# Softmax attention's output computed already turned, its gate turned beforehand, with some PSUM tiles in other banks

## The chip, the cores and the metric

The kernel runs on one core of a Trainium2 chip. The metric is the device time of one execution in microseconds (us), given as the median of the runs. The core's engines run side by side and meet through semaphores: PE (TensorE, matrix products), PEld (its weight loads), DVE (VectorE), ACT (ScalarE), POOL (GpSimd) and SP (SyncE, which here only issues DMAs).

## The reference, cut to what matters

Two decoder layers over 256 tokens of width 1024. Each layer normalises x, multiplies it by one input projection whose 4096 columns are eight groups of 512 (MQ, MK, MV, MZ for softmax attention with 4 heads of 128; RQ, RK, RV, RZ for retention with 4 heads of 128), gates both results with SiLU, multiplies them by an output projection, adds x, and then adds a gated per-layer embedding. With 256 tokens there is one attention block, so the softmax attention is plain causal attention:

```python
pr = softmax(q_m @ k_m.T + bias, causal)       # per head, 256 x 256
m_out = silu(mz) * (pr @ v)                    # per head, 256 x 128
y = concat([r_out, m_out]) @ w_out[i]          # r_out: retention, gated alike
x = x + y
x = x + sigmoid(rms_norm(x) @ w_ple_gate[i]) * rms_norm(p[i] @ w_ple[i], ple_norm_g[i])
```

## The kernel before, in words

**Products.** PE takes a stationary operand of 128 x 128 and a moving one of up to 512 columns. The large products are made of three products of split numbers: each number is a high part (`hi`, type fp32r) and a low part (`lo`, the remainder), and hi·hi, hi·lo and lo·hi are summed in PSUM (`mm3`, lines 405 to 407). Some small products are done in one fp32 product instead, which the profile shows as two records each (lines 950, 960, 1010). Products of split numbers in the attention and retention scores go through `three` (line 932): three records of 256 columns each.

**Weights.** A `Stage` is half of a 512 x 512 weight block's rows in two chunks. Each chunk is loaded by SP (line 340), cast to `hi` by ACT (line 350) and split to `lo` by DVE (line 353), and then used by four `hi`·`lo` products on PE (two row blocks k, two token halves m). There are 95 such chunks; 8 staging buffers and 5 pairs of split buffers hold them, and later in each layer the tiles T, V, G, PS and K2 are lent as further pairs.

**Turning.** A result with tokens on the partitions is wanted with features on the partitions before the next product. `halves` (line 621, ACT) separates the 16-bit halves of the fp32 numbers, `turned` (line 631) lets SP issue a DMA transposition, and two DVE copies (line 640, one for each 16-bit half) put the halves together again. `to_parts` (line 643) does this and then makes `hi` (ACT, line 657) and `lo` (DVE, line 659).

**Order.** The order of the instructions on every engine is fixed when the program is built. A planner (`Flow`) keeps a clock for each engine, takes a cost in us for each step (`ask`), and issues the step that can start first, among several the one with the earliest due time; `LIFT` adds an offset to the due time of chains that it names. The large products follow each other in the order MQ, MK, RQ, RK, MZ, MV, RV, RZ, then the output projection, the embedding (`embed`) and the gate. The small products of attention are `groups` that are put between them (`tick`) when what they need has been ready for a margin and enough `mix` banks are free: `moba_scores`, `moba_out` with `ret_scores_own`, `ret_scores`, `ret_out`.

**Softmax attention.** `moba_scores` makes scores in three tiles; `probs` adds the bias, takes the exponential (sums in `DEN`), and turns the result into `PT` (tile PS), keys on the partitions. `value` copies the projection MV, scaled, to `V`. `moba_out` then calls `pv` for each half m of the tokens: `PT` is stationary, `V` moves, and the output has tokens on the partitions, 12 fp32 products of 128 columns a layer (line 960). `moba_y` multiplies by the gate `G` and by 1/`DEN` with four DVE instructions (line 978), and `to_parts` turns the result and splits it into `yT`, parts 4 to 7, which the output projection reads first. Parts 0 to 3 come from the retention group (`ret_gate`).

**PSUM.** Eight banks: four named `acc` and four named `mix`. The output projection takes all four `acc`, the embedding `mix`.

Of the kernel before, what the change touches and what calls it, by code (L numbers as in the profile page):

```python
# [18 lines left out]
P = 128  # L19
D = 1024  # L20
S = 256
# [37 lines left out]
TURN = 0  # L59
AHEAD = 1.6  # L60
# [5 lines left out]
LIFT = {("gen", 38): 4.0, ("rope", 3): -7.0, ("gen", 4): -4.0, ("gate", 1): 1.0, ("hr1", 3): 2.0}  # L66
# [188 lines left out]
def tile_hybrid_trunk(ctx: ExitStack, tc: tile.TileContext, early, x, pT, ple_g, rel_bias,  # L255
# [332 lines left out]
    L_X = flow.begin(load(lambda: x_t, lambda: x, 1.0), 20.2, 0.0)  # L588
    bd = dram.tile([H, SPAN], F32, name="bd")
# [36 lines left out]
    def turned(u, raw, take=()):  # L626


        yield ask(SP, 1.25, take=("w16",), mb=TURN)
        w = tok_p.tile([P, 2, 4, P], U16, name="w16", bufs=W_BUFS)  # L630
        nc.sync.dma_start(w.rearrange("p t h k -> p (t h) k"), u.rearrange("p t n -> p (t n)"),
                          transpose=True)
        dst = None
        for t in range(2):
            yield ask(DVE, 0.35, take=() if t else take)
            if not t:
                flow.free("u16")
                dst = raw()
            v = dst[:, t]
            nc.vector.tensor_copy(v, w[:, t].rearrange("p (h b) k -> p h (b k)", h=v.shape[1]))  # L640
        flow.free("w16")
# [71 lines left out]
    def embed(l):  # L713
# [7 lines left out]
        def scaled(m, ps):  # L721
            t = small(2, "ssq")
            yield from squares(ps, t)
            s = yield from summed(t)
            r, h = small(1, "er"), small(1, "her")
            yield from rsqrt(r, s, 1.0 / D, 0.55)
            yield ask(DVE, 0.1)
            nc.vector.tensor_scalar(h, r, 0.5, None, op0=ALU.mult)
            for n in range(2):
                sl = slice(n * GW, (n + 1) * GW)  # L730
                yield ask(DVE, 0.665, after=(L_GB[l],))
                nc.vector.scalar_tensor_tensor(E[l][:, m, sl], ps[n], h, gb[:, sl],
                                               op0=ALU.mult, op1=ALU.mult)
                flow.free("mix")

        for m in range(MT):
            ps = [bank(mix_p, "mix") for _ in range(2)]
# [32 lines left out]
    def layer(l, aT):  # L770
# [92 lines left out]
        def value(g, m, ps):  # L863
            yield ask(ACT, 0.585, take=() if m else ("V",), after=need_stats(m) + ((VA[g],) if m else ()))
            if not m:
                V[g] = big.tile([P, MT, GW], F32, name="V", bufs=1)
                flow.reach(VA[g])
            nc.scalar.activation(V[g][:, m], ps, AF.Copy, scale=stats(m)[0 if g == MV else 2])
            flow.free("acc")
# [12 lines left out]
        def after_proj(g, m, ps):  # L882
# [4 lines left out]
            if g == RZ:  # L887
                YC[m, 0] = made(yT, m, 0, c)
# [22 lines left out]
        def probs(m, h0, per, ps):  # L911
# [16 lines left out]
            yield from turned(u, lambda: raw[:, :, h0:h0 + per, m * P:m * P + n])  # L928

        def three(ps, w, x):  # L930
            for i, (a, b) in enumerate(((0, 0), (0, 1), (1, 0))):
                nc.tensor.matmul(ps, w[a], x[b], start=i == 0, stop=i == 2)  # L932

        def moba_scores():
# [17 lines left out]
            for n in ("T", "T", "K2", "Q2"):  # L952
                flow.free(n, flow.clock[PE])

# [9 lines left out]
        yT, YC = Parts(), {}  # L964

        def moba_y(m, ps):
            ri = small(H, "ri")
            yield ask(DVE, 0.1)
# [3 lines left out]
            yield ask(DVE, 0.26, take=("tok",), after=(GC[MZ, m],))  # L972
            y = tok_p.tile([P, GW], F32, name="tok")
            for h in range(H):
                if h:
                    yield ask(DVE, 0.26)
                sl = slice(h * DH, (h + 1) * DH)
                nc.vector.scalar_tensor_tensor(y[:, sl], ps[:, sl], ri[:, h:h + 1], G[MZ][:, m, sl],  # L978
                                               op0=ALU.mult, op1=ALU.mult)
            flow.free("mix")  # L980
            if m:
                flow.free("G")
            u = yield from halves(y, "tok")
            yield from to_parts(yT, m, 4, u)
# [10 lines left out]
        SC, RO, RC = {}, {}, {}  # L995
# [30 lines left out]
        def ret_norm(m, ps):  # L1026
# [23 lines left out]
            RO[m] = o  # L1050

        def ret_out():
            for m in range(MT):
                ps = pv(m, lambda h, m, b: box["ST"][:, h, S:] if b else box["ST"][:, h, m * P:(m + 1) * P], V[RV])
                RC[m] = flow.begin(ret_norm(m, ps), flow.soon(9.6))
# [31 lines left out]
        def both(d, *keys):  # L1087
            return lambda: [d.get((g, m)) for g in keys for m in range(MT)]

        groups.append(([both(TC, MQ, MK), lambda: [L_B]], moba_scores, 3, 2.9))  # L1090
        groups.append(([lambda: [PC.get(k) for k in ((0, 0), (1, 0), (1, 2))], both(VC, MV), both(TC, RQ, RK)],
                       moba_out, 3, 2.0))
        groups.append(([], ret_scores, 2, 2.2))
        groups.append(([lambda: [SC.get(h) for h in ("own", 0, 2)], both(VC, RV)], ret_out, 2, 0.3))
# [40 lines left out]
        def added(m, n, ps):  # L1135
# [3 lines left out]
            flow.free("acc")  # L1139
# [173 lines left out]
```

## Time and profile before

| what | value |
|---|---|
| time, median of 3 runs | 295.98 us |
| lowest and highest run | 295.57 and 296.82 us |
| span of the profiled execution, first to last instruction | 294.1 us |
| busy PE / PEld / DVE / ACT / POOL | 288.9 / 246.5 / 253.5 / 214.7 / 30.9 us |
| DMA packets moved | 69.77 MB |

The time of a run is a little more than the span, since it holds what lies ahead of the first instruction and behind the last. The page gives no separate time for the profiled execution; the median lies 1.9 us above its span. A busy share counts matmuls from start to modelled end, and neighbouring matmuls overlap, so the mean length of a matmul in the groups is longer than the distance at which the next one starts. The chain of work that ended last lists that distance.

### The profile page before, as it was taken

What the parts mean: (1) busy time and instruction counts of PE and PEld (TensorE: products, weight loads), DVE (VectorE), ACT (ScalarE), POOL (GpSimd) and SP (SyncE); (2) the same over time, 40 slices, a digit from 0 to 9 for tenths busy, and PEclk for the clock granted to TensorE, in tenths of its full rate; (3) what the DMA queues carried; (4) which work ended last, traced back from release to release, by engine and by line L of the source; (5) the groups of instructions that cost most, each with busy time, mean ns of one, the idle gap of its engine ahead of it and who ended that gap; (6) DMA issues with size and microseconds to landing.
All of it is one profiled execution on the core that took longest, in us unless ns stands there. A gap on an engine that the chain in (4) does not pass through costs nothing.

```text
span 294.1 us, 4301 instructions
## 1 busy us (share of the span) xinstructions
PE 288.9 (98%) x1411; PEld 246.5 (84%) x1411; DVE 253.5 (86%) x461; ACT 214.7 (73%) x376; POOL 30.9 (11%) x44
## 2 busy tenths in 40 slices
PE   8999999999999999999999999999999999999994
PEld 4788888888899888888888888888898988888884
DVE  3967799999899999699999589999998797969942
ACT  3979974799747893998585896599646869479411
POOL 5004200000001200022003220000000030001300
PEclk9999999999999999999999999999999999999999
DMA  7999999998969868698689969787999766943021
GB/s 220 378 403 410 290 244 309 377 290 187 245 193 270 337 150 280 152 245 319 166 198 296 370 187 220 281 222 170 242 322 243 274 226 176 295 89 71 0 75 71
DMA packets 61774, 69.77 MB, mean 237 GB/s; under 512 B 46260, under 2 KB 47160, under 8 KB 61624
## 3 DMA queue, kind: packets, MB, share of 16 engines
q1 hardware_dynamic: 61712, 69.50, 79.7%
q8 instruction: 11, 0.18, 0.3%
q14 instruction: 11, 0.09, 0.1%
q0 software_dynamic: 32, 0.01, 0.0%
q10 hardware_dynamic: 8, 0.00, 0.0%
HBM read 57.42 MB, written 1.05 MB: 199 GB/s over the span
## 4 chain that ended last, share of the span: by engine, by line
PE 96%; DMA 2%; SPq 0%; ACT 0%; DVE 0%; issue 0%
PE acc L406 26%; PE acc L405 26%; PE acc L407 26%; PE acc L553 4%; PE mix L960 4%; PE mix L932 2%; DMA a<-in_early 2%; PE mix L407 1%; PE mix L743 1%; PE mix L742 1%; PE mix L406 1%; PE mix L744 1%; PE mix L405 1%; PE mix L1010 1%; PE mix L950 1%; ACT wh L459 0%
## 5 line engine op out<-in xcount | busy, mean ns | idle before, releaser
L405 PE MATMUL acc<-wh,a 128*128 128x512 f32 (+1 forms) x286 | 107.8, 377 | 0.0
L406 PE MATMUL acc<-wl,a 128*128 128x512 f32 (+1 forms) x286 | 107.7, 377 | 0.0
L407 PE MATMUL acc<-wh,a 128*128 128x512 f32 (+1 forms) x286 | 107.4, 376 | 0.0
L353 DVE TENSOR_TENSOR wl<-wst,wh 128x1024 fp32r<-128x1024 f32 x76 | 92.0, 1222 | 9.1 <-ACT wh L350 8.9
L350 ACT CAST wh<-wst 128x1024 fp32r<-128x1024 f32 x76 | 78.6, 1054 | 15.2 <-PE acc L407 6.0
L405 PEld LDWEIGHTS acc<-wh,a 128*128 128x128 f32 x286 | 53.5, 187 | 9.1
L407 PEld LDWEIGHTS acc<-wh,a 128*128 128x128 f32 x286 | 53.5, 187 | 9.0
L406 PEld LDWEIGHTS acc<-wl,a 128*128 128x128 f32 x286 | 53.5, 187 | 8.7
L621 ACT COPY u<-tok 128x1024 uint16<-128x1024 uint16 x30 | 31.1, 1053 | 12.7 <-DVE tok L978 7.9
L657 ACT CAST a<-tmp 128x512 fp32r<-128x512 f32 x20 | 12.4, 618 | 10.9 <-DVE tmp L654 8.3
L621 ACT COPY u<-x_t 128x1024 uint16<-128x1024 uint16 x12 | 12.5, 1042 | 10.2 <-DVE x_t L1138 6.8
L673 POOL TENSOR_TENSOR ro<-rs_t,neghalf 128x4 f32<-128x4 f32 x4 | 5.8, 1460 | 129.0 <-DVE rs_t L671 129.0
L640 DVE COPY tmp<-w 128x512 uint16<-128x512 uint16 x40 | 16.4, 466 | 0.1
L659 DVE TENSOR_TENSOR a<-tmp,a 128x512 fp32r<-128x512 f32 x20 | 13.7, 685 | 0.0
L640 DVE COPY T<-w 128x512 uint16<-128x512 uint16 x32 | 12.9, 467 | 0.7 <-DMA w<-u 0.7
L553 PE MATMUL acc<-wh,a 128*128 128x512 f32 (+1 forms) x42 | 11.3, 387 | 0.3 <-ACT wh L459 0.3
L960 PEld LDWEIGHTS mix<-V,PS 128*128 128x128 f32 x96 | 11.3, 192 | 0.3
L1189 DVE SCALAR_TENSOR_TENSOR tmp<-tmp,E 128x512 f32<-128x512 f32 (+1 forms) x9 | 5.7, 629 | 6.7 <-ACT tmp L1183 3.8
L960 PE MATMUL mix<-V,PS 128*128 128x128 f32 x96 | 11.4, 275 | 0.0
L1186 ACT ACTIVATE tmp<-acc,hr 128x512 f32<-128x512 f32 (+1 forms) x8 | 5.0, 631 | 8.5 <-PE acc L407 8.5
L405 PE MATMUL acc<-T,a 128*128 128x512 f32 (+1 forms) x30 | 11.0, 367 | 0.0
L407 PE MATMUL acc<-T,a 128*128 128x512 f32 (+1 forms) x30 | 10.9, 365 | 0.0
(144 smaller groups left out, 458.2 us busy)
## 6 DMA issues: line engine op xcount, KB each, us to landing
wst<-in_w_in SPq DMA_DIRECT2D x59, 512.0 KB, 6.3
wst<-in_w_out SPq DMA_DIRECT2D x16, 512.0 KB, 6.6
wst<-in_w_gate SPq DMA_DIRECT2D x16, 512.0 KB, 4.6
wst<-in_w_ple SPq DMA_DIRECT2D x4, 512.0 KB, 7.6
wst<-in_early SPq DMA_DIRECT2D x4, 384.0 KB, 7.4
a<-in_early SPq DMA_DIRECT2D x3, 384.0 KB, 5.8
x_t<-in_x SPq DMA_DIRECT2D x1, 1024.0 KB
gb<-in_ple_g SPq DMA_DIRECT2D x2, 512.0 KB, 6.7
```

What stands on the lines that cost most here:

```text
L350: nc.scalar.copy(hi, s)
L353: nc.vector.tensor_tensor(lo, s, hi.bitcast(F32), op=ALU.subtract)
L405: nc.tensor.matmul(ps, ah, wh, start=start, stop=False)
L406: nc.tensor.matmul(ps, ah, wl, start=False, stop=False)
L407: nc.tensor.matmul(ps, al, wh, start=False, stop=stop)
L553: nc.tensor.matmul(ps[m][:, sl], (a0.lo if which[0] == "lo" else a0.hi)[:, k, m * P:(m + 1) * P], columns(w, sl), start=start and i + j == ...
L621: nc.scalar.copy(u, src.bitcast(U16).rearrange("p (n t) -> p t n", t=2))
L640: nc.vector.tensor_copy(v, w[:, t].rearrange("p (h b) k -> p h (b k)", h=v.shape[1]))
L657: nc.scalar.copy(h, src)
L659: nc.vector.tensor_tensor(a.lo[:, k0:k0 + 4, m * P:(m + 1) * P], src, h.bitcast(F32), op=ALU.subtract)
L932: nc.tensor.matmul(ps, w[a], x[b], start=i == 0, stop=i == 2)
L960: nc.tensor.matmul(ps[:, h * DH:(h + 1) * DH], lhs(h, m, b), v[:, b, h * DH:(h + 1) * DH], start=b == 0, stop=b == m)
```

## The change

`moba_out` makes the output with features on the partitions: `V` is stationary and `PT` moves, for each head one product of 256 columns over the first half of the keys (split in `hi` and `lo`, three fp32r records) and one fp32 product of 128 columns over the second half of the keys, which only the second half of the tokens needs. For this the first half of `V` and the first half of the keys of `PT` are split; their parts are kept in parts of `yT` that are free until then. The gate with 1/`DEN` is now multiplied and turned by itself (`gate_turned`) into an own tile `GT`, started once gate and probabilities are there, and `moba_y` multiplies the output by it and splits it straight into `yT`.

`turned` joins its two copies into one of 1024 elements. The embedding's first token half takes `acc` banks instead of `mix`, the second column half of the output projection `mix` instead of `acc`. `ret_gate` waits for a mark at the end of `ret_norm` instead of for the chain. `LIFT` gets 12 more entries, two of them margins of groups.

```diff
+GATES = 6.0
-LIFT = {("gen", 38): 4.0, ("rope", 3): -7.0, ("gen", 4): -4.0, ("gate", 1): 1.0, ("hr1", 3): 2.0}
+LIFT = {('gen', 38): 4.0, ('rope', 3): -7.0, ('gen', 4): -4.0, ('gate', 1): 1.0, ('hr1', 3): 2.0, ('ret_scores', 0): 1, ('gen', 49): -6, ('moba_out', 0): 0.5, ('hr1', 1): -6, ('gen', 18): 1.5, ('gen', 19): 1.5, ('gen', 20): 1.5, ('gen', 21): 1.5, ('ret_tanh', 1): 4, ('ret_norm', 0): -6, ('gen', 34): -4}
...
+    gt = ct.tile([P, H, S], F32, name="GT")
...  turned
-        for t in range(2):
-            yield ask(DVE, 0.35, take=() if t else take)
...
-            nc.vector.tensor_copy(v, w[:, t].rearrange("p (h b) k -> p h (b k)", h=v.shape[1]))
+        yield ask(DVE, 0.62, take=take)
+        flow.free("u16")
+        dst = raw()
+        nc.vector.tensor_copy(dst, w.rearrange("p t (h b) k -> p t h (b k)", h=dst.shape[2]))
...  embed
-            ps = [bank(mix_p, "mix") for _ in range(2)]
+            ps = [bank(mix_p, "mix") if m else bank(acc_p, "acc") for _ in range(2)]
...  value
+            if m or g == RV:
+                nc.scalar.activation(V[g][:, m], ps, AF.Copy, scale=scale)
+            else:
+                hi, lo = box["VT"] = [yT.both[:, k].rearrange("p t s -> p (t s)") for k in (6, 7)]
+                nc.scalar.activation(hi, ps, AF.Copy, scale=scale)
+                yield ask(DVE, 0.665)
+                nc.vector.scalar_tensor_tensor(lo, ps, scale, hi.bitcast(F32), op0=ALU.mult, op1=ALU.subtract)
...  probs
+            src, hi, lo = (v[:, h0:h0 + per, m * P:(m + 1) * P] for v in (box["PT"], yT.hi, yT.lo))
+            yield ask(ACT, 0.1 + 0.11 * per)
+            nc.scalar.copy(hi, src)
+            yield ask(DVE, 0.08 + 0.13 * per)
+            nc.vector.tensor_tensor(lo, src, hi.bitcast(F32), op=ALU.subtract)
...
+        def gate_turned(m):
+            ri = small(H, "ri")
+            yield ask(DVE, 0.1, after=(GC[MZ, m], *PC.values()))
+            nc.vector.reciprocal(ri, DEN[m])
+            yield ask(DVE, 0.14)
+            nc.vector.tensor_scalar(ri, ri, stats(m)[1], None, op0=ALU.mult)
+            yield ask(DVE, 0.605, take=("tok",))
+            o = tok_p.tile([P, GW], F32, name="tok")
+            nc.vector.tensor_tensor(o.rearrange("p (h d) -> p h d", h=H), G[MZ][:, m].rearrange("p (h d) -> p h d", h=H),
+                                    ri[:, :, None].to_broadcast([P, H, DH]), op=ALU.mult)
...
+            u = yield from halves(o, "tok")
+            raw = gt.bitcast(U16).rearrange("p h (k t) -> p t h k", t=2)
+            yield from turned(u, lambda: raw[:, :, :, m * P:(m + 1) * P])
+        def moba_y(i, ps):
+            yield ask(DVE, 0.605, take=("tmp",), after=tuple(GTC[m] for m in range(MT)))
+            t = tmp_p.tile([P, GW], F32, name="tmp").rearrange("p (h s) -> p h s", h=2)
+            nc.vector.tensor_tensor(t, ps.rearrange("p (h s) -> p h s", h=2), gt[:, i::2], op=ALU.mult)
+            flow.free("mix")
+            yield ask(ACT, 0.53)
+            hi, lo = (v[:, H + i::2] for v in (yT.hi, yT.lo))
+            nc.scalar.copy(hi, t)
+            yield ask(DVE, 0.605)
+            nc.vector.tensor_tensor(lo, t, hi.bitcast(F32), op=ALU.subtract)
+            flow.free("tmp")
         def moba_out():
-            for m in range(MT):
-                ps = pv(m, lambda h, m, b: box["PT"][:, h, (m + b) * P:(m + b + 1) * P], V[MV])
-                YC[m, 4] = made(yT, m, 4, flow.begin(moba_y(m, ps), flow.soon(3.1)))
+            vh, vl = box["VT"]
+            banks = [bank(mix_p, "mix") for _ in range(2)]
+            for h0 in range(0, H, 2):
+                heads = [(h, slice(h * DH, (h + 1) * DH), banks[h - h0][:, h0 * P:h0 * P + S]) for h in range(h0, h0 + 2)]
+                for h, d, o in heads:
+                    flow.row(0.342)
+                    three(o, [v[:, d] for v in (vh, vl)], [v[:, h] for v in (yT.hi, yT.lo)], False)
+                for h, d, o in heads:
+                    flow.row(0.22)
+                    nc.tensor.matmul(o[:, P:], V[MV][:, 1, d], box["PT"][:, h, S:], start=False, stop=True)
...  ret_norm, at its end
+            flow.reach(RN[m])
...  ret_gate
-            while m not in RC:
-                yield ask(DVE, 0.0)
-            yield ask(DVE, 0.605, take=("tok",), after=(RC[m],))
+            yield ask(DVE, 0.605, take=("tok",), after=(RN[m],))
...  output projection
-                        acc[m][n] = bank(acc_p, "acc")
+                        acc[m][n] = bank(mix_p, "mix") if n else bank(acc_p, "acc")
```

More of the change, by code (lines that the diff above doesn't have):

```diff
@@ L733, in scaled @@
                                                op0=ALU.mult, op1=ALU.mult)
-                flow.free("mix")
+                flow.free("mix" if m else "acc")
         for m in range(MT):
-            ps = [bank(mix_p, "mix") for _ in range(2)]
+            ps = [bank(mix_p, "mix") if m else bank(acc_p, "acc") for _ in range(2)]
             for n in range(2):
@@ L863, in value @@
         def value(g, m, ps):
-            yield ask(ACT, 0.585, take=() if m else ("V",), after=need_stats(m) + ((VA[g],) if m else ()))
-            if not m:
+            first = m == (g == MV)
+            yield ask(ACT, 0.585, take=("V",) if first else (),
+                      after=need_stats(m) + ((VA[g],) if m and g == RV else ()))
+            scale = stats(m)[0 if g == MV else 2]
+            if first:
                 V[g] = big.tile([P, MT, GW], F32, name="V", bufs=1)
                 flow.reach(VA[g])
-            nc.scalar.activation(V[g][:, m], ps, AF.Copy, scale=stats(m)[0 if g == MV else 2])
+            if m or g == RV:
[5 more added lines that the diff above has]
+                nc.vector.scalar_tensor_tensor(lo, ps, scale, hi.bitcast(F32), op0=ALU.mult, op1=ALU.subtract)
             flow.free("acc")
@@ L887, in after_proj @@
             if g == RZ:
-                YC[m, 0] = made(yT, m, 0, c)
+                made(yT, m, 0, c)
+            if g == MZ:
+                turn_gates()
         def project(gs, by_m=False, pre=None):
@@ L928, in probs, with three @@
             yield from turned(u, lambda: raw[:, :, h0:h0 + per, m * P:m * P + n])
-        def three(ps, w, x):
+            src, hi, lo = (v[:, h0:h0 + per, m * P:(m + 1) * P] for v in (box["PT"], yT.hi, yT.lo))
[3 more added lines that the diff above has]
+            nc.vector.tensor_tensor(lo, src, hi.bitcast(F32), op=ALU.subtract)
+        def three(ps, w, x, stop=True):
             for i, (a, b) in enumerate(((0, 0), (0, 1), (1, 0))):
-                nc.tensor.matmul(ps, w[a], x[b], start=i == 0, stop=i == 2)
+                nc.tensor.matmul(ps, w[a], x[b], start=i == 0, stop=stop and i == 2)
         def moba_scores():
@@ L962, in pv, with turn_gates @@
             return ps
-        yT, YC = Parts(), {}
-        def moba_y(m, ps):
+        yT = Parts()
+        GTC = {}
+        def turn_gates():
+            for m in range(MT):
+                if (MZ, m) in GC and (m, 2 * m) in PC and m not in GTC:
+                    GTC[m] = flow.begin(gate_turned(m), flow.soon(GATES))
+        def gate_turned(m):
             ri = small(H, "ri")
-            yield ask(DVE, 0.1)
+            yield ask(DVE, 0.1, after=(GC[MZ, m], *PC.values()))
             nc.vector.reciprocal(ri, DEN[m])
@@ L971, in moba_y @@
             nc.vector.tensor_scalar(ri, ri, stats(m)[1], None, op0=ALU.mult)
[L972 to L979, printed above, removed]
@@ new lines, in moba_out @@
+        def moba_out():
+            vh, vl = box["VT"]
[8 more added lines that the diff above has]
+                    nc.tensor.matmul(o[:, P:], V[MV][:, 1, d], box["PT"][:, h, S:], start=False, stop=True)
+            for i, ps in enumerate(banks):
+                c = flow.begin(moba_y(i, ps), flow.soon(3.1))
+                for m in range(MT):
+                    for k in range(H + i, KT, 2):
+                        yT.made[m, k] = c
@@ L992, in moba_out @@
             ret_scores_own()
-        SC, RO, RC = {}, {}, {}
+        SC, RO, RN = {}, {}, [Mark() for _ in range(MT)]
         def decayed(h0, n, cols, ps):
@@ L1138, in added @@
             nc.vector.tensor_tensor(xs, ps, xs, op=ALU.add)
-            flow.free("acc")
+            flow.free("mix" if n else "acc")
             u = yield from halves(xs, None)
```

19 lines of the change are left out of this document (6 added, 13 removed).

## The prediction

> **What bounds the kernel now.** I read the page first: the span, the busy shares, and the chain that ended last.
>
> ```profile
> span 294.1 us, 4301 instructions
> PE 288.9 (98%) x1411; PEld 246.5 (84%) x1411; DVE 253.5 (86%) x461; ACT 214.7 (73%) x376; POOL 30.9 (11%) x44
> PE 96%; DMA 2%; SPq 0%; ACT 0%; DVE 0%; issue 0%
> ```
>
> The chain is PE nearly from end to end, so I looked at its ends and its pace in the chain in order of time (start, length, what), and at all waits of PE.
>
> ```profile
> 8.64 10.42 PE acc L553 x46
> 28.08 0.22 PE mix L407
> 28.74 0.22 PE mix L407
> 290.04 0.48 ACT tmp L1186
> ...
> PE mix L295 <- PEq L1302: 0.8, 1, 0.8
> PE acc L553 <- ACT wh L459: 0.3, 1, 0.3
> ```
>
> PE waits twice, both times in the first 9 us, while the first blocks arrive. From 8.64 to 290.04 us it issues without a wait, one group of three 512-column matmuls every 0.66 us (28.08 to 28.74). Behind 290.04 stand 4.1 us of tail (294.1 - 290.04), which the change leaves alone. So the time falls only by PE work that disappears, and rises by any wait that the change brings to PE. An engine that is merely full costs nothing until then. The windows show how full they are (PE, PEld, DVE, ACT busy):
>
> ```profile
> 50.00:80.00 30.00, 30.00 (x148) 25.81 (x148) 28.82 (x45) 24.72 (x42) 0.00 (x0) 1.00 0.96 281
> 187.00:217.00 30.00, 30.00 (x148) 25.80 (x147) 29.89 (x46) 25.49 (x42) 0.00 (x0) 1.00 0.83 225
> 217.00:235.00 18.00, 18.00 (x117) 16.40 (x116) 14.74 (x36) 11.11 (x14) 0.00 (x0) 1.00 0.87 274
> ```
>
> DVE is nearly full in the 30 us before the attention output of each layer (28.8 and 29.9 of 30), just where the change puts new DVE work, and it has 3.3 us free in the 18 us behind it in layer 1.
>
> **PE's part.** The chain gives the issue time of the products concerned: the old attention output (line 960, first and third row of the fence), and records of 256 columns of split numbers, once behind an fp32 product and once behind an fp32r one.
>
> ```profile
> 79.46 2.68 PE mix L960 x24
> 82.14 0.89 PE mix L1010 x8
> 217.49 2.68 PE mix L960 x24
> ...
> 50.32 1.39 PE mix L932 x12
> 84.36 1.38 PE mix L932 x12
> ```
>
> - Gone, per layer: 12 fp32 products, 24 records, 2.68 us.
> - New: four heads of three fp32r records with 256 columns. That is the form of line 932, 12 records, 1.38 us.
> - New: four fp32 products of 128 columns, 8 records. That is the form of line 1010, 0.89 us.
> - Switches between fp32 and fp32r: two more per layer than before. The 12 records behind an fp32 product took 1.39, the others 1.38, so a switch costs about 0.01 us.
>
> 1.38 + 0.89 + 0.02 - 2.68 = -0.39 us a layer, -0.8 us in all. Writing two banks in turn, the other unknown, is shown by no row. Line 932 too fills more than one bank, so I take 0; if each of four bank changes a layer cost as much as a type switch, it were 0.1 us in all, and a gain has no reason.
>
> **DVE's part.** Pieces of DVE's timeline, rows of groups, and the three groups of the copies that are joined:
>
> ```profile
> 71.48 1.30 DVE L802 TENSOR_TENSOR K<-T,K 128x512 fp32r<-128x512 f32 x2
> 196.06 1.51 DVE L640 COPY T<-w 128x512 uint16<-128x512 uint16 x4
> 218.48 0.17 DVE L969 RECIPROCAL ri<-den 128x4 f32<-128x4 f32 x1
> 218.68 0.23 DVE L971 TENSOR_SCALAR ri<-ri,hr 128x4 f32<-128x4 f32 x1
> 219.03 1.13 DVE L978 SCALAR_TENSOR_TENSOR tok<-mix,ri,G 128x128 f32<-128x128 f32 x4
> ...
> L878 DVE SCALAR_TENSOR_TENSOR G<-tmp,acc 128x512 f32<-128x512 f32 x4 | 2.8, 693 | 0.0
> L640 DVE COPY tmp<-w 128x512 uint16<-128x512 uint16 x40 | 16.4, 466 | 0.1
> L640 DVE COPY T<-w 128x512 uint16<-128x512 uint16 x32 | 12.9, 467 | 0.7 <-DMA w<-u 0.7
> L640 DVE COPY PS<-w 128x512 uint16<-128x512 uint16 x12 | 4.8, 477 | 0.8 <-DMA w<-u 0.8
> ```
>
> Back to back, a 512-column tensor_tensor costs 0.65 us, a copy 0.38, a 128-column gate step 0.28.
>
> New before the attention output, per layer: the low part of the probabilities, one of 0.65 and two of half that size, between 0.33 and 0.65 each (I take 0.33, since the 128-column step costs 0.28 and the 512-column one 0.65: the cost goes with the size); the low part of V, 0.69 by line 878. Moved there: for each token half 0.17 + 0.23, a gate product of 0.65 and the copies of its turning, 0.76. That is 0.65 + 0.66 + 0.69 + 2 x 1.81 = 5.6 us a layer (6.3 with the upper price).
>
> Gone from behind it: the same 0.4 and 0.76 per half, and four gate steps (1.13) against one product of 0.65. That is 2 x (0.4 + 0.76 + 1.13 - 0.65) = 3.3 us; the low part of y (0.65 per half) stays. Net +2.3 us a layer.
>
> Against that stand 42 joined copies (84 rows now, 40 + 32 + 12). One copy of 1024 elements lies between the price of one copy of 512, 0.38, and that of two, 0.76. I take 0.76, because the number of elements is the same; the range is then 0 to 16 us of DVE time given back.
>
> [...] No row here has the larger copy.
>
> **What hides it.** DVE work costs nothing while the weight chunks stay ahead of PE. Each chunk feeds four hi·lo products, so counting both sides gives the lead. The first fence counts weight splits on DVE begun by a time, lines 406 and 743 on PE, and the next product; the second is the same for layer 0, where line 743 has not run.
>
> ```profile
> 0.00:199.30 199.30, 79.51 (x66) 1.00 0.90 267
> 0.00:203.00 203.00, 96.05 (x252) 47.32 (x253) 1.00 0.90 267
> 0.00:203.00 203.00, 3.05 (x8) 1.50 (x8) 1.00 0.90 267
> 203.02 0.38 PE L406 MATMUL acc<-wl,a 128*128 128x512 f32 x1
> ```
>
> ```profile
> 0.00:64.60 64.60, 22.80 (x19) 1.00 1.00 327
> 0.00:68.95 68.95, 27.44 (x72) 13.65 (x73) 1.00 0.99 318
> 68.96 0.38 PE L406 MATMUL acc<-wl,a 128*128 128x512 f32 x1
> ```
>
> In layer 1, 252 + 8 = 260 products have used 65 chunks by 203.00, and the 66th, whose split ended by 199.3, is needed at 203.02: a lead of 3.7 us. In layer 0, 72 products have used 18 chunks, and the 19th, done by 64.6, is needed at 68.96: 4.4 us. These are the smallest leads that I found in the two stretches. The 5.6 us come in pieces between splits, over some 20 us, so I cost them at nothing; if this cover is gone they cost what exceeds the lead. ACT gets three casts a layer more, of the probabilities, and has 4.5 us free in the fullest 30.
>
> **New waits.** `moba_y` now waits on DVE for both turned gates; behind it in DVE's order stand weight splits. The two transpositions of the gate move on SP's queue from behind the attention output to ahead of it, past weight loads.
>
> ```profile
> DVE PS L640 <- DMA w<-u: 0.8, 1, 0.8
> ...
> 69.86 2.62 SPq L631 DMA_TRANSPOSE w<-u  x2
> 84.20 4.00 SPq L631 DMA_TRANSPOSE w<-u  x2
> ```
>
> The longest wait of DVE for a transposition is 0.8 us, under the lead of 3.7 us, so I cost that wait at nothing. The two issues hold SP for 2.6 us; a load behind them comes later by as much, still less than the lead, though more than half of it. The banks (`acc` and `mix` exchanged) and the due times only move who waits for whom off PE, where no wait exists to be won.
>
> **The sum.** Span 294.1 - 0.8 = 293.3. The median of the runs lies 1.9 us above the profiled span (295.98 - 294.1), which stays: 295.2 us.
>
> **The rivals.**
>
> *Waits eat the gain.* The leads shrink in both layers and PE stands for about 0.4 us in each: 295.2 + 0.8 = 296.0. For it: DVE at 29.9 of 30 and SP past its loads. Against it: the smallest leads are 3.7 and 4.4 us, and DVE may get time back from the joined copies.
>
> *Slower: the split behind the pile.* In each layer the 5.6 us of new and moved DVE work is issued ahead of the chunk with the smallest lead. PE then stands 5.6 - 3.7 = 1.9 us in layer 1 and 5.6 - 4.4 = 1.2 in layer 0: 295.2 + 3.1 = 298.3. It decides once the waits of PE together exceed 0.8 us, and it shows in a measurement above 2.3. For it: both stretches are full already. Against it: the pieces become ready one after another, behind the exponential, the gate and V, not at once, and 3.3 us are free right behind the output.
>
> *The matmuls are not the bound.* If PE had room to take in more, removing issue time would remove nothing: 296.0. PEld is busy for 84% only. Against it: every matmul of the chain starts one issue distance behind the last, and PE waits for nothing. [...]
>
> *Faster than the sum.* New due times would have to shorten the start, the only place where PE waits after its first matmul: 0.3 us, so 294.9.
>
> **How the numbers follow.** A difference of about 0.5% (1.5 us) is what a measurement of this kernel can tell from no change; its three runs spread over 1.25 us (295.57 to 296.82). Chances: the forecast 0.62, waits that eat the gain 0.18, the slower case 0.12, the matmuls not the bound 0.03, faster than the sum 0.05. The first two, and all but part of the last two, lie within 0.5% of 295.98, because the whole of the removable work is 0.27%: same 0.80. Faster by over 0.5% needs 1.5 us, more than the sum and the start's wait together: 0.07, for the spread of runs alone. Slower by over 0.5%: 0.13, the slower case with a little of the waits. The range reaches down by the start's wait and half a spread, to 294.3, and up to half way between the rivals of 296.0 and 298.3, 297.2; the upper half of the slower case is left out.
>
> **What would show it.** Right: PE's list of waits unchanged, PE in the chain from some 8.6 to 289.2 us, the new products with 12 + 8 records in about 2.3 us, DVE still below its 253.5 plus 5 us, leads above 2 us in the two stretches. The joined copy's mean tells whether the join gives DVE time back. Wrong: any new wait of PE for DVE, ACT or a DMA; above all one before lines of weight products between 60 and 80 or 190 and 225 us, with DVE full ahead of it.

## The result, and the profile after

The changed kernel takes 299.68 us (median of 6 runs, 297.29 to 300.25) against 296.12 (6 runs of the kernel before beside it). The ratio is 1.0097, 95% interval 1.0074 to 1.0121: slower, and outside the predicted range. The profiled run took 300.25 us with a span of 298.3 us, 4.2 us longer than before's span. The page of after, its head and the chain by engine:

```profile
span 298.3 us, 4237 instructions
PE 291.6 (98%) x1403; PEld 248.1 (83%) x1403; DVE 256.3 (86%) x419; ACT 216.5 (73%) x382; POOL 31.6 (11%) x44
PE 78%; DVE 12%; DMA 6%; issue 2%; ACT 1%; DVEq 0%
```

The chain, PE at 96% before, now runs through DVE for 12%. The lines of the code have moved: the weight split is line 354, its cast 351, the joined copy 638, the split products 406 to 408, the retention output 975, the decays (DVE's products of the retention's scores with a table) 1044, the multiplication by the gate (`moba_y`) 1010, its low part 1016. PE's waits, and its timeline around the two outputs of layer 0 (start, length, what, and in brackets the wait before it and its releaser):

```profile
PE mix L975 <- DVE PS L1044: 1.9, 1, 1.9
PE mix L296 <- PEq L1346: 0.8, 1, 0.8
...
82.50 0.87 PE L946 MATMUL mix<-a 128*128 128x256 f32 x6
84.81 1.06 PE L1055 MATMUL mix<-T 128*128 128x128 f32 x8
89.69 1.78 PE L946 MATMUL mix<-K,Q 128*128 128x256 f32 x12
92.44 0.39 PE L408 MATMUL acc<-wh,a 128*128 128x512 f32 x1
94.75 4.54 PE L975 MATMUL mix<-V,PS 128*128 128x128 f32 x24 [1.92 <-DVE PS L1044]
99.05 0.47 PE L406 MATMUL acc<-wh,a 128*128 128x512 f32 x1
```

The new output takes 84.81 - 82.50 = 2.31 us, as worked out (1.38 + 0.89 + 0.02 = 2.29). But then PE waits 1.92 us for the retention's decays, and the 24 records behind that wait take 99.05 - 94.75 = 4.30 us. Before, they took 92.17 - 89.57 = 2.60 us from the same start to the same next start:

```profile
89.57 2.84 PE L960 MATMUL mix<-V,PS 128*128 128x128 f32 x24
92.17 0.47 PE L405 MATMUL acc<-wh,a 128*128 128x512 f32 x1
```

The windows of after say why (length, then PE, PEld, DVE, ACT and POOL busy, the mean granted clock as a share of PE's full clock, DMA's busy share and GB/s):

```profile
92.00:95.00 3.00, 1.08 (x6) 0.65 (x5) 3.00 (x5) 2.67 (x3) 0.00 (x0) 1.00 1.03 422
95.00:98.00 3.00, 3.00 (x16) 3.00 (x16) 1.57 (x11) 0.00 (x0) 0.00 (x0) 0.50 0.52 190
```

Right behind the stretch in which PE was idle its clock was halved. So the 4.2 us are 1.9 (wait) + 1.7 (half clock, 4.30 - 2.60) - 0.7 (PE's work) + 1.3, the rest, in pieces of at most 0.4 us. What DVE did meanwhile:

```profile
84.53 1.37 DVE L638 COPY GT<-w 128x1024 uint16<-128x1024 uint16 x2
85.79 2.34 DVE L354 TENSOR_TENSOR wl<-wst,wh 128x1024 fp32r<-128x1024 f32 x2
88.05 0.68 DVE L765 TENSOR_TENSOR pl<-pf,ph 128x512 fp32r<-128x512 f32 x1
88.65 1.22 DVE L354 TENSOR_TENSOR wl<-wst,wh 128x1024 fp32r<-128x1024 f32 x1
89.79 1.28 DVE L1010 TENSOR_TENSOR tmp<-mix,GT 128x512 f32<-128x512 f32 x2
90.98 0.68 DVE L1044 TENSOR_TENSOR PS<-mix,cst 128x512 f32<-128x512 f32 x1
91.58 1.28 DVE L1016 TENSOR_TENSOR a<-tmp,a 128x512 fp32r<-128x512 f32 x2
92.78 1.22 DVE L354 TENSOR_TENSOR wl<-wst,wh 128x1024 fp32r<-128x1024 f32 x1
93.92 1.28 DVE L1044 TENSOR_TENSOR PS<-mix,cst 128x512 f32<-128x512 f32 x2
```

DVE has no gap. The gate is turned by 85.9 and the output is there by 85.0, but `moba_y` starts at 89.79, behind three weight splits and a split of the embedding's input; the last two decays (the scores for them ended at 91.3) stand behind the low part of y and one more split. Counting splits begun and lo products issued, as in the prediction, shows when those splits are needed:

```profile
0.00:79.90 79.90, 27.78 (x23) 1.00 1.00 304
0.00:80.00 80.00, 33.41 (x88) 1.00 1.00 304
0.00:88.20 88.20, 32.56 (x27) 1.00 1.00 303
0.00:99.30 99.30, 38.01 (x100) 0.98 0.97 302
```

88 products by 80.00 have used 22 chunks; the 23rd was split by 79.9: its lead has sunk to 0.2 us. But 100 products by 99.3 have used 25: the 26th and 27th were ready by 88.2, 11 us or more ahead of their use. Work that nobody needs for 11 us stands ahead of work that PE waits for.

In layer 1 PE lists no such wait, but only just: the last two decays run from 237.43 to 238.72 there, and the retention output begins at 238.27.

### The profile page after: what moved, and what is told of

Its sections match the earlier page's. It is cut to its first block, busy times and chain, and to the rows that moved or that the text cites. A ratio compares the mean times of both kernels' runs of the same rounds, so it can differ in the third digit from the quotient of the medians.

```text
span 298.3 us, 4237 instructions
## 1 busy us (share of the span) xinstructions
PE 291.6 (98%) x1403; PEld 248.1 (83%) x1403; DVE 256.3 (86%) x419; ACT 216.5 (73%) x382; POOL 31.6 (11%) x44
## 4 chain that ended last, share of the span: by engine, by line
PE 78%; DVE 12%; DMA 6%; issue 2%; ACT 1%; DVEq 0%
PE acc L406 18%; PE acc L408 18%; PE acc L407 18%; PE acc L554 5%; DVE wl L354 5%; DMA w<-u 3%; PE mix L406 3%; PE mix L408 3%; PE mix L407 3%; PE mix L975 3%; DMA wst<-in_w_in 2%; DVE T L638 1%; PE mix L946 1%; PE mix L296 1%; PE mix L740 1%
## 5 line engine op out<-in xcount | busy, mean ns | idle before, releaser
L406 PE MATMUL acc<-wh,a 128*128 128x512 f32 (+1 forms) x270 | 102.1, 378 | 0.0
L408 PE MATMUL acc<-wh,a 128*128 128x512 f32 (+1 forms) x270 | 101.7, 377 | 0.0
L407 PE MATMUL acc<-wl,a 128*128 128x512 f32 (+1 forms) x270 | 101.2, 375 | 0.0
L408 PEld LDWEIGHTS acc<-wh,a 128*128 128x128 f32 x270 | 50.5, 187 | 8.8
L407 PEld LDWEIGHTS acc<-wl,a 128*128 128x128 f32 x270 | 50.5, 187 | 8.6 <-DVE wl L354 0.2
L406 PEld LDWEIGHTS acc<-wh,a 128*128 128x128 f32 x270 | 50.5, 187 | 8.3 <-DVE G L885 0.3
L623 ACT COPY u<-x_t 128x1024 uint16<-128x1024 uint16 x12 | 12.5, 1044 | 11.5 <-DVE x_t L1182 5.9
L406 PE MATMUL mix<-wh,a 128*128 128x512 f32 x40 | 15.2, 381 | 0.0
L408 PE MATMUL mix<-wh,a 128*128 128x512 f32 x40 | 15.2, 381 | 0.0
L407 PE MATMUL mix<-wl,a 128*128 128x512 f32 x40 | 15.2, 379 | 0.0
L638 DVE COPY T<-w 128x1024 uint16<-128x1024 uint16 x16 | 12.2, 771 | 1.8 <-DMA w<-u 1.7
L638 DVE COPY tmp<-w 128x1024 uint16<-128x1024 uint16 x16 | 12.3, 771 | 0.8 <-DMA w<-u 0.7
L554 PE MATMUL acc<-wh,a 128*128 128x512 f32 (+1 forms) x42 | 11.8, 405 | 0.0
L657 DVE TENSOR_TENSOR a<-tmp,a 128x512 fp32r<-128x512 f32 x16 | 10.9, 683 | 0.0
L933 ACT ACTIVATE tok<-tok,nm 128x128 f32<-128x128 f32 (+1 forms) x16 | 7.1, 446 | 5.1 <-DVE nm L930 5.1
```

Of the source, the lines that this page charges most:

```text
L406: nc.tensor.matmul(ps, ah, wh, start=start, stop=False)
L407: nc.tensor.matmul(ps, ah, wl, start=False, stop=False)
L408: nc.tensor.matmul(ps, al, wh, start=False, stop=stop)
L554: nc.tensor.matmul(ps[m][:, sl], (a0.lo if which[0] == "lo" else a0.hi)[:, k, m * P:(m + 1) * P], columns(w, sl), start=start and i + j == ...
L623: nc.scalar.copy(u, src.bitcast(U16).rearrange("p (n t) -> p t n", t=2))
L638: nc.vector.tensor_copy(dst, w.rearrange("p t (h b) k -> p t h (b k)", h=dst.shape[2]))
```

## The experiments

Theory A: DVE, which works through a fixed order, comes late to the decays of layer 0 through the low parts and the early gate, and PE waits. Its rivals: the clock alone; the new order and due times rather than the work; the turned output in either layer. Each result is a median, then its ratio to the kernel before, timed beside each run, with the 95% interval of the ratio. The diffs are cut to the lines that matter.

**A reorder, a filler, and the decays late by themselves.** Low part of y behind the decays; nine dummy products of ones ahead of the retention output; in the kernel before, seven dummy DVE products ahead of the decays.

```diff
 e1, moba_y, layer 0            (DM: marks at the end of the last two decays)
-            yield ask(DVE, 0.605)
+            yield ask(DVE, 0.605, after=() if l else DM)
 e2, pv
+            if l == 0 and m == 0:
+                for _ in range(9):
+                    nc.tensor.matmul(ps, ones[:, :P], ones, start=True, stop=True)
 e3, kernel before, decayed
+            if l == 0 and n == 2 and not h0:
+                for _ in range(7):
+                    nc.vector.tensor_tensor(scr, dec[:, :2], dec[:, :2], op=ALU.mult)
```

> The kernel after, with one thing moved on DVE in layer 0: the two low parts of y (2 x 0.64 us) behind the two decays that the retention output waits for; PE's order is the same. Theory A (the retention output of layer 0 waits 1.9 us for decays that stand behind work on DVE that nobody needs yet, and the idle PE then gets half its clock for 3.4 us): the wait shrinks by 1.28 to about 0.6 us, the 24 records behind it take 2.7 us instead of 4.5, the run takes about 297. Rival B (DVE has too much work in all, the wait is only where it shows): another wait of PE takes its place, 299 or more. Rival C (the half clock has nothing to do with the wait): the records still take 4.5 us, 298.4.

> The kernel after, with nine 512-column bf16 products of ones put on PE ahead of the retention output of layer 0, into the bank that the output then overwrites; every other engine has the same order. They fill 1.9 us that PE stands there. Theory A: the decays come no sooner, so the retention output starts at the same time, but PE is never idle, the clock stays whole, the 24 records take 2.7 us: 298.5 or a little less than that, and the runs spread less. Rival C: the clock halves all the same, 300.

> The kernel before, with seven DVE products of 128x512 (0.6 us each, into a tile that nobody reads) ahead of the first of the two decays of layer 0; nothing of the change, PE's order is that of before. There the last decay ended 2.0 us ahead of the retention output; now it ends 4.2 us later. Theory A: PE waits 2.2 us at the retention output, and the clock halves for 3.4 us in some runs or all: 298.3 without and 300.0 with the half clock. Rival C: PE waits 2.2 us and the clock stays whole in every run, 298.3. If a wait of this length were hidden elsewhere: 296.1.

Measured: e1 298.32 us, 1.0059 (1.0036 to 1.0082); e2 298.38, 1.0063 (1.0038 to 1.0088); e3 300.88, 1.0158 (1.0118 to 1.0198). PE's waits in e1, DVE's line that explains it, and PE's waits in e3:

```profile
PE mix L975 <- DVE PS L1046: 1.8, 1, 1.8
```

```profile
91.98 1.22 DVE L354 TENSOR_TENSOR wl<-wst,wh 128x1024 fp32r<-128x1024 f32 x1 [1.04 <-ACT wh L351]
93.13 1.28 DVE L1046 TENSOR_TENSOR PS<-mix,cst 128x512 f32<-128x512 f32 x2
```

```profile
PE mix L961 <- DVE PS L1003: 2.5, 1, 2.5
PE acc L405 <- DVE tok L1080: 0.5, 1, 0.5
PE acc L407 <- DVE a L660: 0.4, 1, 0.4
```

e1 leaves the wait as it was (0.6 us was expected): a split whose cast came late took the place of the low part. Its profiled run has no half clock behind the wait (its mean clock is 0.997), to which the last section comes back. e2 fills PE's wait with work: no half clock in any of its 6 runs (mean clock 0.999 or 1.000), and by the ratios some 1.0 us less than after (the two intervals overlap). It is still 1.9 us slower than the kernel before; so the clock is the smaller part of the loss, and what PE waits for (here covered with ones) the larger. e3 makes the old kernel slow in the same place with late decays alone (300.88 us, for 300.0 at most expected), and shows a second place: the output projection, which waits for the retention's gate product (0.5 us) and the low part of its y (0.4 us).

**Moving the wait.** A larger margin for the retention output; then, in e1, the late split held behind the decays too.

```diff
 e4, LIFT
+ ('ret_out', 0): 3.0
 e5, e1 and in Stage            (DM0: the marks of e1)
-            yield ask(DVE, 1.135)
+            yield ask(DVE, 1.135, after=DM0 if 2 * self.i + c == 33 else ())
```

> The kernel after, with 3 us added to the margin of the retention output of layer 0, so that PE goes on with large products and takes it up four groups of three products later; the planner moves other steps as it follows. Theory A: the decays are done by then, PE does not wait there and keeps its clock, and the shorter attention output remains as a gain of 0.8: 295.3 to 295.9. Rival B: PE waits elsewhere in layer 0, 297 or more.

> As the kernel of e1 (the two low parts of y behind the decays), and the one weight split that stood ahead of the two decays in layer 0 moved behind them too; the planner shifts some later steps as it follows. In e1 that split waited 1.0 us for its cast and took 1.2 us with the decays behind it. Theory A, mended (DVE takes its queue in order; what stands ahead of the decays, the split and its late cast, is the price): the last decay ends 2.2 us sooner, PE waits 0.3 us or not at all at the retention output of layer 0, no half clock: the kernel before less about 0.4, 296.3 on a chip where that takes 296.7. Rival B (too much DVE work in all): the split or something behind it comes late for PE instead, 298 or more.

e4 307.05 us, 1.0358 (1.0331 to 1.0385), a plain miss; e5 298.22, 1.0059 (1.003 to 1.0088). Waits in e4, then in e5:

```profile
PE acc L406 <- ACT a L655: 3.7, 3, 2.6
PE acc L408 <- DVE a L657: 2.2, 3, 1.0
```

```profile
PE acc L410 <- DVE a L659: 1.5, 1, 1.5
```

In both the wait at the retention output is gone, and PE waits for the low or high part of the retention's y at the output projection, in e4 also in layer 1. In the kernel before that low part ended at 110.49, some 0.5 us ahead of the weight load that reads it (110.96); a later retention output uses that up.

```profile
109.81 0.68 DVE L659 TENSOR_TENSOR a<-tmp,a 128x512 fp32r<-128x512 f32 x1
```

**Parts of the change undone.** Two copies in place of the joined one; the due times of before (the change adds 11 entries to `LIFT`, not 12); the low parts of probabilities and V left out, so that the products read the high parts in their place and the output lacks that precision.

```diff
 e6, turned
-        nc.vector.tensor_copy(dst, w.rearrange("p t (h b) k -> p t h (b k)", h=dst.shape[2]))
+        for t in range(2):
+            nc.vector.tensor_copy(dst[:, t], w[:, t].rearrange("p (h b) k -> p h (b k)", h=dst.shape[2]))
 e7: LIFT as before
 e8, value and probs
-                nc.vector.scalar_tensor_tensor(lo, ps, scale, hi.bitcast(F32), op0=ALU.mult, op1=ALU.subtract)
-            nc.vector.tensor_tensor(lo, src, hi.bitcast(F32), op=ALU.subtract)
```

> The kernel after with the joined copy of 1024 elements made as two of 512 again, in every turning; every engine's order is the same. By the rows (0.65 us for a joined one back to back, 0.70 to 0.76 for two) DVE gets 0.05 to 0.1 us more work at each of some seven turnings in the stretch ahead of the retention output of layer 0. Theory A: the wait there grows by 0.4 to 0.7 us, the time by as much or, where the half clock comes more often, by up to 1: 299.5 to 300.5. If the join gives nothing: as the kernel after.

> The kernel after with the due times and margins of the kernel before (the 12 new entries taken out); the products, the banks and the joined copies are those of after. On DVE one decay of layer 0 then stands ahead of the weight split and the other behind it. Theory A: the wait at the retention output of layer 0 is there all the same, between 1 and 3 us, so about the time of after, 298 to 301. Rival D (the new due times, not the new work, make DVE late): no wait there, 296 to 297.

> The kernel after with the low parts of the probabilities and of V left out: three DVE instructions for the probabilities and one for V a layer are not done, and the products that would read them read the high parts, so PE's, ACT's and SP's orders and PE's work are the same and the output lacks that precision. DVE has 2.3 us less to do ahead of the retention output of layer 0. Theory A (the DVE work that the change adds there makes the decays late): the decays end 2.3 us sooner, PE does not wait there, the clock stays whole, and the shorter attention output shows as a gain: the time before less 0.4 to 0.8, 295.9 to 296.3 on a chip where that takes 296.7. Rival D (the order, not the added work): a wait of 1 us or more stays.

e6 301.0 us, 1.0151 (1.0112 to 1.019); e7 301.26, 1.0152 (1.0109 to 1.0194); e8 297.07, 1.0016 (0.9995 to 1.0036). By the ratios the joined copies and the new due times each save about 1.6 us of the changed kernel's time (uncertain by 1.3 each), and the low parts, 2.3 us of DVE a layer, cost 2.4 in all (uncertain by 0.9). e8 falls between its two forecasts: less work helps, but a wait is left and nothing is gained on the kernel before. e7 shows only that the old due times are worse still, not that the new order is good. PE's wait in e8:

```profile
PE mix L973 <- DVE PS L1042: 0.9, 1, 0.9
```

**One layer at a time, and the rest without the output.** A switch chooses the old or the new attention output by layer (`TURNED`); due times as in after (e9, e10) or as before (e11, e12).

```diff
-            if m or g == RV:
+            if m or g == RV or l not in TURNED:
...
-                       moba_out, 3, 2.0 + LIFT.get(("moba_out", l), 0.0)))
+                       moba_out if l in TURNED else old_out, 3, 2.0 + LIFT.get(("moba_out", l), 0.0)))
 e9: TURNED = (1,)   e10: TURNED = (0,)   e11: TURNED = ()   e12: TURNED = (1,)
```

> The kernel after, but with the turned output, its split probabilities and V and its early gate in layer 1 alone; layer 0 makes its attention output the old way (tokens on the partitions, gate behind it), with the joined copies, the banks and the due times of the change. Theory A (all of the loss is one layer 0 matter: DVE without a gap for 32 us, so the chain from attention output to retention output comes late): no wait of PE at layer 0's retention output, no half clock, layer 1's product cheaper by 0.4 us: 295.4 to 296.0 against 296.1 before. Rival B (the turned output costs in each layer): half of the loss stays, 297.9. Rival C (due times and banks bring the loss, not the output): 299 to 300.

> The complement: the turned output in layer 0 alone, layer 1 the old way, everything else as in the kernel after. Theory A: as slow as the kernel after, 299 to 300, with PE's wait of 1 to 2 us for the decays ahead of layer 0's retention output. Rival B: 297.9. Rival C: 299 to 300 too, so that this run tells A from B and the one with layer 1 alone tells A from C.

> The kernel before with only the joined copies, the exchanged banks and the mark in the retention's gate: no turned output in either layer and the due times of before. DVE loses about 42 times 0.1 us, 4 us, of work. Theory A: PE waited for nothing before, so that gives no time: 295.6 to 296.4. Rival (DVE was a bound in the kernel before already): faster by up to 2 us, 294 to 295.

> The turned output in layer 1 alone with the due times of the kernel before, joined copies and banks as in the change: the candidate that could beat both kernels. Theory A: 295.3 to 295.9, no wait of PE between 60 and 120 us, at most 0.4 us of waits in layer 1. If layer 1 needs the new due times, it has waits there of 1 us or more and comes to 297.

e9 297.23 us, 1.0015 (0.9999 to 1.0032); e10 299.52, 1.0097 (1.007 to 1.0124), as slow as the whole change, with the wait of 1.5 us for the decays: the loss is layer 0's. But e9 gains nothing on the kernel before either. e11 was a miss: 298.89, 1.0075 (1.0055 to 1.0095), without any turned output; and e12 298.95, 1.0074 (1.005 to 1.0098), with a wait of 1.7 us at the same place as e11. Waits of e9 (both at layer 0's retention output, which is made the old way there, so due times, copies or banks bring them), then the wait of e11, DVE's lines of e11 at that place and those of before:

```profile
PE mix L978 <- ACT V L871: 1.2, 1, 1.2
...
PE mix L978 <- DVE PS L1075: 0.4, 1, 0.4
```

```profile
PE acc L409 <- DVE a L658: 1.7, 1, 1.7
```

```profile
148.01 0.68 DVE L1264 SCALAR_TENSOR_TENSOR tmp<-tmp,E 128x512 f32<-128x512 f32 x1
...
149.34 1.22 DVE L355 TENSOR_TENSOR wl<-wst,wh 128x1024 fp32r<-128x1024 f32 x1
150.47 0.68 DVE L658 TENSOR_TENSOR a<-tmp,a 128x512 fp32r<-128x512 f32 x1
```

```profile
145.19 1.22 DVE L353 TENSOR_TENSOR K<-wst,K 128x1024 fp32r<-128x1024 f32 x1
146.33 0.69 DVE L659 TENSOR_TENSOR a<-tmp,a 128x512 fp32r<-128x512 f32 x1
```

At 149 us, where layer 1 begins, a split stands ahead of the low part that PE waits for. It does so in the kernel before too. What is new in e11 are the embedding's two steps (lines 1264 and 1266, 148.01 to 149.41), which stand ahead of both; before, they came behind the low part, from 146.93 on. The planner makes a new order from the new costs; that the old due times suit only the old costs is likely, but not shown.

**Is it DVE's time or its order?** Low parts and gate product moved to POOL (e13) or the gate product alone (e15), order unchanged; the kernel before with joined copies in its own order (e14); then after without three splits or one (e16, e17: the low part is replaced by the high one), order unchanged.

```diff
 e13, probs and gate_turned (e15: the second alone)
-            nc.vector.tensor_tensor(lo, src, hi.bitcast(F32), op=ALU.subtract)
+            nc.gpsimd.tensor_tensor(lo, src, hi.bitcast(F32), op=ALU.subtract)
-            nc.vector.tensor_tensor(o.rearrange("p (h d) -> p h d", h=H), G[MZ]
+            nc.gpsimd.tensor_tensor(o.rearrange("p (h d) -> p h d", h=H), G[MZ]
 e14, kernel before, turned: both steps are still asked for, then
+        nc.vector.tensor_copy(dst, w.rearrange("p t (h b) k -> p t h (b k)", h=dst.shape[2]))
 e16, Stage; NO_LOW = (18, 19, 20), in e17 (19,)
+            if self.split[0] in NO_LOW:
+                lo = hi
```

> The kernel after with the same order of instructions on PE, DVE, ACT and SP, but the three low parts of the probabilities and the two gate products of each layer run on POOL, which is idle there. DVE has 2 x 1.36 us less to do ahead of layer 0's retention output. Theory A (DVE's time in the full stretch is the cause): the wait of 1.9 us at the retention output goes or falls under 0.5 us, no half clock: 295.5 to 297. Rival (the order and the due times are the cause, not DVE's time): the waits stay and the time with them, 299 to 300. Either falls if POOL is so slow that the attention output itself waits for it; the wait would then name POOL.

> The kernel before with only the two copies of each turning made one, in the order of before (the planner still reckons two): no bank, mark, due time or product changed. DVE has some 42 x 0.1 us less to do. If the slowness of the kernel with copies and banks alone came from the order that the planner made of the new costs (a weight split ahead of the copy at 145 us), this one has no new wait: 295.4 to 296.4. If the joined copy itself delays a chain (the first half is no longer ready early), it has waits and comes to 297 or more.

> As the kernel with both moved to POOL, but the two gate products alone: half of the relief, 1.36 us a layer. Theory A: about half of the loss is left, the wait at layer 0's retention output between 0.4 and 1.2 us and no half clock: 297 to 298.5. Rival (order): 299 to 300.

> The kernel after with the same order of instructions, but three of the weight splits on DVE between 66 and 75 us in layer 0 are left out (3.6 us of DVE's time; the four products of each of these chunks that would use the low part read the high part, so PE's work is the same). Theory A (DVE's time ahead of layer 0's outputs is the cause): the waits at 92 us go, and the time falls to that of the kernel before less PE's 0.8 us: 295.3 to 296.3. Rival (the order and the due times, not DVE's time): 298.5 to 300.

> The same with a single split left out, 1.2 us of DVE's time, at 69 us. Theory A: between the kernel after (299.7) and the one with the low parts left out (2.3 us of DVE's time, 297.07), with PE's wait at layer 0's retention output at 0.7 us or less and no half clock: 297.5 to 298.7. Rival: 298.5 to 300, wait 1.5 to 2 us.

e13 301.2 us, 1.0155 (1.0128 to 1.0182); e15 301.25, 1.0156 (1.0132 to 1.0181); e14 296.44, 0.9992 (0.9973 to 1.001); e16 298.03, 1.006 (1.0034 to 1.0085); e17 298.05, 1.004 (1.0014 to 1.0065).

e14 clears the joined copy: DVE does 1.3 us less (252.2 against 253.5), PE lists no wait behind its first 9 us, the time is the same. e11's loss is therefore one of order or banks. e13 and e15 did not test what they were meant to, since DVE was not relieved (256.8 and 256.5 us busy, 256.3 in after); that is told in the last section. In e16 3.6 us of work vanished between 66 and 75 us, but the last two decays began only 0.95 us earlier (92.97 for 93.92) and PE's wait stayed at 1.8, because DVE then waited for others and PE itself came there 0.8 us earlier. DVE of e16:

```profile
67.93 0.69 DVE L890 SCALAR_TENSOR_TENSOR G<-tmp,acc 128x512 f32<-128x512 f32 x1 [0.63 <-ACT tmp L886]
69.38 0.69 DVE L947 TENSOR_TENSOR a<-PS,a 128x512 fp32r<-128x512 f32 x1 [0.77 <-ACT a L945]
70.48 0.78 DVE L643 COPY PS<-w 128x1024 uint16<-128x1024 uint16 x1 [0.41 <-DMA w<-u]
```

What counts is DVE's work behind the last probabilities (73 us), not the sum over the stretch. e8 fits this: of the 2.27 us that it leaves out in layer 0, 1.59 lie at 72.9 us and behind, and its last decays begin 1.3 us earlier (92.60). So theory A's "too much work" falls as a sum over the stretch. e17's median lies in the band of A, but its profiled run has the full wait of 1.9 us, and the four slowest of its 12 runs (299.03 to 299.48 us) show a mean clock of 0.991 or 0.992, so it decides nothing.

**Only the order.** Eleven splits of layer 0 may not begin earlier than 8 us before their use by the planner's clock, and e1's edit; PE's order is that of after.

```diff
 e18, Flow.can and Stage
+        if eng == DVE and hasattr(c, "cap"):
+            r = max(r, c.due() + 5.7 - c.cap)
+                    if 30 <= 2 * self.i + c <= 40:
+                        self.chains[c].cap = 8.0
```

> The kernel after, PE's order unchanged, but in layer 0 eleven weight splits (chunks 30 to 40 of the input order) may begin on DVE at the earliest 8 us before PE needs them by the planner's clock (in the kernel after, those that stand ahead of the gate multiplication and of the decays end 12 to 15 us before their use), and the low part of y comes behind the decays. Theory A' (DVE is late only because work that is not due for 12 us and more stands ahead of the chain from attention output to retention output): no wait of PE at 92 us, none at the output projection at 110 to 117 us, no half clock: 294.9 to 296.2, so at least as fast as the kernel before. Rival (DVE has too much to do in the whole stretch from 62 to 120 us, whatever its order): the waits come back at the retention's y or at the deferred splits between 100 and 125 us, 1.5 us or more, and the time is 297.5 to 300.

297.46 us, 1.003 (1.0009 to 1.005), no half clock in the profile (mean 1.000). PE's waits and DVE's timeline of e18:

```profile
...
PE mix L411 <- DVE wl L358: 0.7, 1, 0.7
PE acc L410 <- ACT a L659: 0.4, 1, 0.4
```

```profile
86.84 0.68 DVE L1014 TENSOR_TENSOR tmp<-mix,GT 128x512 f32<-128x512 f32 x1
89.96 1.40 DVE L1050 TENSOR_TENSOR PS<-mix,cst 128x512 f32<-128x512 f32 x2 [0.72 <-PE mix L950]
108.57 0.69 DVE L661 TENSOR_TENSOR a<-tmp,a 128x512 fp32r<-128x512 f32 x1
```

The same work on PE in the same order, and on DVE in another (ACT's order shifts with it): the last two decays begin at 89.96, 4.0 us earlier, and now DVE waits for PE; the wait at the retention output is gone and the low part of y is ready at 109.3, before 110.5. Against after's ratio of 1.0097, two thirds of the loss are won back, and the two intervals do not overlap. The time is 1.3 us above the forecast of A', whose other wait came: 0.7 us for a deferred split at 113 us, where the rival's mechanism shows at a smaller size. A wait of 0.4 us at 159 us, in layer 1, is for a high part that ACT makes. So it is mostly order, with too little room to spare. No version beat the kernel before; an order fitted beyond e18 wasn't tried.

## Why the prediction was wrong, point by point

- **PE's part: right.** 2.31 us measured for 2.29, in both layers, so PE's own work falls by 2.68 - 2.31 = 0.37 us a layer, 0.7 in all. No price for changing banks showed.
- **DVE's part: right in size.** The low parts measure 0.68 + 0.42 + 0.43 + 0.74 = 2.27 us in layer 0 (2.0 assumed), DVE's total 256.3 (253.5 and at most 5 expected). Two joined copies take 85.79 - 84.53 = 1.26 us, 0.63 each, below the 0.76 taken. But e14 shows that in the kernel before, where PE did not wait for DVE, the gift is worth nothing.
- **"What hides it": the step that failed.** The lead of the weight chunks was taken as the whole cover of DVE's added work, and the 5.6 us were costed at nothing. For the chunks that held: no PE wait for a split is listed, though their lead fell to 0.2 us in layer 0 and 0.5 in layer 1, below the 2 us that were to show the step right. What was left out are the leads of the small chains. The decays had 89.73 - 85.74 = 4.0 us between the retention's scores and its output before, 18 products of 512 columns. In after 6 such products stand there, 92.66 - 91.31 = 1.35 us (92.66 is one product behind 92.44); with the old due times (e7) it is 12. The retention's y had 0.5 us. So 5.6 us were put into an order where small chains stand behind splits, the last two decays began at 93.92, and PE waited 1.9 us.
- **New waits.** It was said that weight splits stand behind `moba_y`; the trace has them ahead of it, for 3.9 us, and it's these that e18 moves.
- **Banks and due times "move who waits for whom off PE".** Wrong in both directions: e7 shows 1.6 us saved by the new due times, e11 2.2 us lost with copies and banks under the old ones.
- **The rivals.** "The split behind the pile", 298.3 at 0.12, has the right engine and nearly the right size, but it priced the split as the victim, in both layers; here the splits are the pile, and all of it lies in layer 0 (e9, e10). The clock was in no rival: 1.7 of the 4.2 us, and its share differs by run (three of the six runs of after show a mean clock of 0.991 or 0.992, the profiled one among them). Even without it (e2, 298.38 us) the time lies above the range.
- **What would show it wrong** was named: a new wait of PE for DVE with DVE full ahead. It came at 92 us, just behind the stretch that the prediction watched, and before small products, not weight products.

## What to carry to other kernels

Before calling added work on a full in-order engine free, list every consumer that PE meets in the next 30 us, the small products above all, with its own lead; the smallest lead counts, with the work that is queued in front of it. When such a chain is late, look first for work in front of it that is not due for long. Here moving that won back two thirds of the loss with all the work kept (e18), and leaving out the low parts, most of which lie behind 72 us, helped about as much (e8), but leaving out more work further ahead left the wait as it was (e16). When two versions differ in work, an order that suits the one can be a handicap of the other (e7, e11), so a version has to be judged with an order of its own.

## What the runs showed of the hardware

- **The clock after idle time.** In the profile of after PE's granted clock was 0.50 from 95.02 to 98.43 us, for 3.41 us, and again from 296.41 us on, 197.98 us or 58 such lengths after the end of the first. In the 3.41 us ahead of the first (91.61 to 95.02) PE was busy for 1.49 us and idle for 1.92, ahead of the second (293.00 to 296.41) busy for 1.28 and idle for 2.13. In e5 the clock was 0.50 from 113.40 to 116.80 us, behind waits of 0.23 and 1.50 us between 110.7 and 113.2, and in e4 from 260 to 266 us, behind 4 us with 2.64 of idle (256 to 260). A wait of about this length was not always followed by a half clock: 3.41 us of it lower the mean by 0.006 (0.5 x 3.41 / 298.3), but the profiled runs with waits of 1.8 us (e1), 1.9 (e6 and e13) and 2.5 (e3) have means of 0.997, 0.997, 1.000 and 1.000. The 58 whole lengths fit a grid of 3.41 us, and the author's estimate was that idle time counts within one stretch of it; where these stretches lie in e1, e3, e6 and e13 is not shown, so why their clock stayed whole is open.
- **DVE beside POOL.** In e13 POOL's 512-column subtraction took 1.81 us where DVE took 0.68, and DVE's own instructions became longer beside it: a 4-column step 1.03 us for 0.23, a split 2.05 for 1.22. Over the whole run the four 4-column steps have a mean of 0.57 us (0.23 in after). POOL's spans are rough in these profiles. POOL and DVE of e13:

```profile
71.01 1.81 POOL L942 TENSOR_TENSOR a<-PS,a 128x512 fp32r<-128x512 f32 x1 [36.61 <-ACT a L940]
78.43 2.60 POOL L998 TENSOR_TENSOR tok<-G,ri 128x512 f32<-128x512 f32 x2 [1.52 <-DVE ri L993]
```

```profile
78.47 1.03 DVE L995 TENSOR_SCALAR ri<-ri,hr 128x4 f32<-128x4 f32 x1
80.06 2.05 DVE L354 TENSOR_TENSOR wl<-wst,wh 128x1024 fp32r<-128x1024 f32 x1
```

  DVE's busy time stayed at 256.8 us (256.3 in after) with 10 instructions fewer. What made its instructions longer, no view here shows.
